# A block of unread products behind the last product of a streaming-encoder layer

## The chip, the core and the metric

The kernel runs on one core of a Trainium2 chip. TensorE (PE in the profile) multiplies a stationary operand, the weights, which is loaded into its array first (PEld), with a moving operand that is streamed through it column by column; results go into PSUM, eight accumulator banks. VectorE (DVE), ScalarE (ACT) and GpSimd (POOL) do everything elementwise; SyncE (SP) issues most of the DMAs. The metric is the device time of one execution in microseconds. Both kernels compute the same output; the change adds work whose results nothing reads.

## The reference

One layer on an input of 512 positions with 1024 channels, all in float32:

```python
h = rms_norm(x, norm_mix)
u_pool, u_lru, q, k, v, g_logits = split(h @ w_in)        # 8192 columns
gates = sigmoid(g_logits + b_gate)                        # three times 1024
y_pool = pool_mixer(u_pool)       # windows 2/4/8/16, grouped linear map
y_lru  = rglru_mixer(u_lru)       # causal convolution, gated scan over positions
y_sb   = stick_breaking_attention(rms_norm(q), rms_norm(k), v)   # 8 heads of 128
merged = gates0 * (y_pool @ wb0) + gates1 * (y_lru @ wb1) + gates2 * (y_sb @ wb2)
x = x + merged @ w_out
h2 = rms_norm(x, norm_ffn)
x = x + (silu(h2 @ w_gate) * (h2 @ w_up)) @ w_down        # 2816 hidden columns
```

## The kernel before

Everything is kept with channels on the 128 partitions and the 512 positions along the free dimension. A float32 matrix product is made of three products in the faster 32-bit matmul type float32r: each operand is split into a high part (a cast on ScalarE, L141, L1462) and a low part (the difference, on VectorE, L142, L1463), and high times high, high times low and low times high are accumulated (`mm3`, L304, and `product`, L310). In the attention's projection, in one branch and in the feed-forward part, the products of 2 by 2 blocks are made by a scheme with seven block products in place of eight; that is where the names "11", "S1" to "S4" and "22" come from.

The moving operand is not read in the order of its columns. `il` and `il2` (L94, L111) take the columns of the first and the second half of a block in turn, and whoever reads the result from PSUM puts them back in order:

```python
    def il2(ap):                                          # L111
        return ap.rearrange("p (a b) -> p b a", a=2)
```

So with 256 columns, neighbours in the stream lie 128 columns apart. The weights are always 128 neighbouring columns of a tile, such as `a_[a][:, w, k0 + k, :]`.

The last part is the down projection (L1681 on). For each of seven block products `nm` and both halves `q` of the output, `piece` (L1670) runs through three sets of weights and issues for each its products:

```python
                for k in range(nk):                       # L1675
                    for i, (a, b) in enumerate(((0, 0), (0, 1), (1, 0))):
                        nc.tensor.matmul(o, a_[a][:, w, k0 + k, :], il2(b_[b][:, k, :]),
                                         start=first and i == k == 0,
                                         stop=last and i == 2 and k == nk - 1, skip_group_check=True)
```

The sets of weights are prepared ahead by `make_d` (L1597): a cast `whd` or `whdS` on ScalarE and a difference `wld` or `wldS` on VectorE, each into one of a few rotating buffers, so the cast waits until TensorE has used up an older set. The very last piece, ("22", 1), is split by its two output blocks (L1686): after each, VectorE adds the result to the output tile (L1694) and SyncE stores it (L1652). The PSUM tiles `ps_dx`, `ps_dy` come from the pool `fp` with four tiles of two banks each; tiles of 128 by 1024 words in SBUF come from a rotating pool through `g4` (L1322). The framework that builds the program orders the instructions of each engine by priorities and sets the waits; each engine then works through its own list in order.

Of the kernel before, what the change touches and what calls it, by code (L numbers as in the profile page):

```python
# [8 lines left out]
F32 = mybir.dt.float32  # L9
F32R = mybir.dt.float32r  # L10
BF16 = mybir.dt.bfloat16
AF = mybir.ActivationFunctionType
# [4 lines left out]
P = 128  # L17
S = 512
# [46 lines left out]
def layer_kernel(ctx: ExitStack, tc: tile.TileContext, x, xt, vecs, w_in, w_qkv7, w_gate7, w_pool, w_rg, w_ig,  # L65
                 w_branch, w_br7, w_out, w_fg, w_fu, w_fd, w_fd7, out):
    nc = tc.nc
    act = nc.scalar.activation
    dve = nc.vector

    cst = ctx.enter_context(tc.tile_pool(name="cst", bufs=1))
    mp = ctx.enter_context(tc.tile_pool(name="mp", bufs=4))
# [46 lines left out]
    def two2(ap):  # L119
        if ap.shape[-1] == H:  # L120
            return ap.rearrange("p w (a b) -> p w a b", a=2)
        return ap.rearrange("p w (c a b) -> p (w c) a b", c=2, a=2)
# [314 lines left out]
    with ExitStack() as first:  # L437
# [288 lines left out]
        for k in range(KT):  # L726
            if k % 2 == 0:
                wh, wl = weights("first", k // 2)
            for w, x_ in ((wh, 0), (wl, 0), (wh, 1)):
                for n in range(4):  # L730
                    nc.tensor.matmul(pss[n // 2][n % 2], w[:, k % 2, n * P:(n + 1) * P], il(hu[k][x_]),  # L731
                                     start=k == 0 and w is wh and x_ == 0,
                                     stop=k == KT - 1 and x_ == 1)
# [46 lines left out]
        def store(t, i, j, r):  # L780
            nc.gpsimd.dma_start(rows(t, i, j), r)
# [115 lines left out]
        for cc in range(2):  # L897
# [14 lines left out]
            for nm in ORDER:  # L912
                ps, half, first_, t, ts_, src, ss = plan[nm]
# [328 lines left out]
    fp = ctx.enter_context(tc.tile_pool(name="fp", bufs=4, space=PSUM, reuse_waits="tile"))  # L1242
# [4 lines left out]
    with ExitStack() as third:  # L1247
# [42 lines left out]
        for u, nm in BORDER:  # L1290
# [5 lines left out]
            b = BH[nm]  # L1296
            for w in range(2):
                o = ps[:, w, half * H:(half + 1) * H]
                for k in range(4):
                    for n, (x_, y_) in enumerate(((0, 0), (0, 1), (1, 0))):  # L1300
                        nc.tensor.matmul(o, ah[x_][:, w, k, :], il2(b[k][y_]), start=first_ and n == k == 0,  # L1301
                                         stop=n == 2 and k == 3, skip_group_check=True)
# [16 lines left out]
    with ExitStack() as ffn:  # L1319
        gp = ffn.enter_context(tc.tile_pool(name="gp", bufs=GBUFS))  # L1320

        def g4(shape, name, dt=F32):  # L1322

            return gp.tile([P] + shape, dt, tag="g", name=name)
# [13 lines left out]
        for c in range(4):  # L1338
# [10 lines left out]
            for j in range(2):  # L1349
# [3 lines left out]
                t = x1p[c // 2, j][:, c % 2, :]  # L1353
# [112 lines left out]
        acts = []  # L1466
# [61 lines left out]
        for c in range(NDIRECT):  # L1528
# [4 lines left out]
            a = g4([2, S], f"act{c}")  # L1533
# [24 lines left out]
        for m in range(4):  # L1558
            t = fp.tile([P, 2, S], F32, tag="mm", name=f"ps_d{m}")
# [72 lines left out]
        for e in range(2):  # L1632
# [5 lines left out]
            for j in range(4):  # L1638
                m = 4 * e + j
# [41 lines left out]
        for nm in DORDER:  # L1681
# [3 lines left out]
            for q in range(2):  # L1685
                if (nm, q) == ("22", 1):  # L1686

                    make_d(len(dsets))
                    for w, ps in enumerate((XY[1, "y"], XY[0, "x"])):
# [3 lines left out]
                        t = two2(x1p[q, 1][:, ws, lo])  # L1693
# [15 lines left out]
                if nm == "22":  # L1709
                    store(q, 1, lo)  # L1710


_INS = ["x", "xt", "vecs", "w_in", "w_qkv7", "w_gate7", "w_pool", "w_rg", "w_ig", "w_branch", "w_br7", "w_out",
        "w_ffn_gate", "w_ffn_up", "w_ffn_down", "w_down7"]
# [43 lines left out]
```

## Time and profile before

| | us |
|---|---|
| time, median of two runs without profile | 868.24 (867.44 to 869.04) |
| span of the profiled execution, from its first to its last instruction | 866.1 |
| TensorE busy, products | 859.3 |
| TensorE busy, weight loads | 790.0 |
| VectorE busy | 735.4 |
| ScalarE busy | 523.1 |
| GpSimd busy | 91.1 |

The page gives a span for the profiled execution and no other time of it; the runs without profile are 2.1 us above it in the median. A row of the timeline has the start and the duration of an instruction in microseconds, engine, line, operation, `out<-in` by the program's names (for a product first the moving operand, then the weights), its shape, and in brackets how long its engine had been idle and who ended that. A matmul's duration is the time through the pipeline, with an end that is modelled, so the pace of TensorE is read from start to start. A group row has count, least, median and largest duration in ns, then the first and the last start.

### The profile page before, as it was taken

How to read it: one execution, taken by the hardware profiler on the slowest of the kernel's cores; microseconds unless marked ns; L12 is line 12 of the kernel's file. 1: busy time of each engine (PE TensorE's matmuls, PEld its weight loads, DVE VectorE, ACT ScalarE, POOL GpSimd, SP SyncE). 2: the span in 40 equal slices, each digit the busy share in tenths (PEclk: the TensorE clock that was granted, in tenths of full speed). 3: DMA queues.
4: the chain of work that ended last, by engine and by line, in shares of the span. 5: the costliest groups of instructions: out<-in, count | busy, mean ns of one | idle time of the engine just before them, and what ended most of it. 6: DMA issues, size and time to landing. Idle time of an engine off the chain costs nothing.

```text
span 866.1 us, 14232 instructions
## 1 busy us (share of the span) xinstructions
PE 859.3 (99%) x5563; PEld 790.0 (91%) x5563; DVE 735.4 (85%) x937; ACT 523.1 (60%) x727; POOL 91.1 (11%) x130
## 2 busy tenths in 40 slices
PE   9999999999999999999999999999999999999998
PEld 7888878888899988889889988889999999999998
DVE  7899897998796598967898786699988888899974
ACT  6554989556966567546665545465555555755642
POOL 1110002132433101000001100000000000121200
PEclk9999999999999999999999999999999999999999
DMA  9586346899592876735726955345533433797913
GB/s 340 160 284 208 101 156 186 225 315 264 172 313 74 240 222 195 243 119 157 222 87 169 202 165 172 101 139 148 159 110 98 122 99 123 225 243 195 197 42 122
DMA packets 116643, 154.08 MB, mean 178 GB/s; under 512 B 8160, under 2 KB 90080, under 8 KB 116576
## 3 DMA queue, kind: packets, MB, share of 16 engines
q1 hardware_dynamic: 103904, 107.30, 38.8%
q0 software_dynamic: 12528, 45.62, 22.2%
q8 instruction: 43, 0.70, 0.3%
q10 hardware_dynamic: 144, 0.26, 0.1%
q14 instruction: 24, 0.20, 0.1%
HBM read 132.71 MB, written 18.87 MB: 175 GB/s over the span
## 4 chain that ended last, share of the span: by engine, by line
PE 92%; ACT 4%; DVE 2%; issue 1%; DMA 0%; SPq 0%; DVEq 0%; ACTq 0%
PE ps_y L315 11%; PE ps_q L828 8%; PE ps_x L315 8%; PE ps_dy L1677 6%; PE ps_dx L1677 5%; PE ps_br L306 3%; PE ps_br L308 3%; PE ps_br L307 3%; PE ps_gate L731 3%; PE ps_bY L1301 2%; PE ps_gy L315 2%; PE ps_bX L1301 2%; PE ps_gx L315 2%; PE ps_pool L306 2%; PE ps_pool L307 2%; PE ps_pool L308 2%
## 5 line engine op out<-in xcount | busy, mean ns | idle before, releaser
L141 ACT ACTIVATE whi<-raw 128x1024 fp32r<-128x1024 f32 x69 | 72.8, 1055 | 81.7 <-PE ps_br L307 17.1
L142 DVE TENSOR_TENSOR wlo<-raw,whi 128x1024 fp32r<-128x1024 f32 x69 | 84.2, 1220 | 25.6 <-ACT whi L141 25.0
L142 DVE TENSOR_TENSOR wlo<-qw,whi 128x1024 fp32r<-128x1024 f32 x48 | 58.4, 1220 | 17.0 <-ACT whi L141 17.0
L141 ACT ACTIVATE whi<-qw 128x1024 fp32r<-128x1024 f32 x48 | 50.3, 1053 | 26.4 <-PE ps_q L828 11.9
L1462 ACT ACTIVATE wh_S<-w_S 128x1024 fp32r<-128x1024 f32 x36 | 38.4, 1066 | 28.6 <-PE ps_y L315 20.0
L1583 POOL DMA_DIRECT2D dw<-in_w_down_dram x20 | 17.0, 864 | 305.3 <-DVE wl L1463 242.6
L1463 DVE TENSOR_TENSOR wl_S<-w_S,wh_S 128x1024 fp32r<-128x1024 f32 x36 | 43.8, 1218 | 3.3 <-ACT wh_S L1462 3.3
L1462 ACT ACTIVATE wh<-w 128x1024 fp32r<-128x1024 f32 x27 | 28.6, 1060 | 29.3 <-PE ps_x L315 9.4
L1463 DVE TENSOR_TENSOR wl<-w,wh 128x1024 fp32r<-128x1024 f32 x27 | 32.9, 1219 | 7.8 <-ACT wh L1462 7.8
L1462 ACT ACTIVATE whdS<-dw 128x1024 fp32r<-128x1024 f32 x20 | 21.2, 1062 | 20.3 <-PE ps_dy L1677 10.6
L1113 DVE TENSOR_TENSOR_SCAN E<-K,ahead 128x512 f32<-128x512 f32 (+3 forms) x32 | 25.4, 813 | 5.7 <-ACT K L1109 5.6
L1463 DVE TENSOR_TENSOR wldS<-dw,whdS 128x1024 fp32r<-128x1024 f32 x20 | 24.2, 1220 | 4.9 <-ACT whdS L1462 4.9
L306 PE MATMUL ps_lru<-HH,whi 128*128 128x512 f32 x64 | 24.6, 384 | 0.0
L306 PE MATMUL ps_br<-yph,whi 128*128 128x512 f32 x64 | 24.5, 383 | 0.0
L306 PE MATMUL ps_pool<-HH,whi 128*128 128x512 f32 x64 | 24.5, 383 | 0.0
L306 PE MATMUL ps_br<-yHH,whi 128*128 128x512 f32 x64 | 24.5, 383 | 0.0
L306 PE MATMUL ps_gate<-HH,whi 128*128 128x512 f32 x64 | 24.4, 381 | 0.0
L307 PE MATMUL ps_lru<-HL,whi 128*128 128x512 f32 x64 | 24.3, 379 | 0.0
L308 PE MATMUL ps_lru<-HH,wlo 128*128 128x512 f32 x64 | 24.3, 379 | 0.0
L307 PE MATMUL ps_gate<-HL,whi 128*128 128x512 f32 x64 | 24.3, 379 | 0.0
L308 PE MATMUL ps_gate<-HH,wlo 128*128 128x512 f32 x64 | 24.3, 379 | 0.0
L307 PE MATMUL ps_pool<-HL,whi 128*128 128x512 f32 x64 | 24.3, 379 | 0.0
(740 smaller groups left out, 3437.2 us busy)
## 6 DMA issues: line engine op xcount, KB each, us to landing
raw<-in_w_in_dram SPq DMA_DIRECT2D x31, 512.0 KB, 5.2
qw<-in_w_qkv_dram SPq DMA_DIRECT2D x24, 512.0 KB, 6.9
dw<-in_w_down_dram POOLq DMA_DIRECT2D x20, 512.0 KB, 8.5
w<-in_w_ffn_gate_dram SPq DMA_DIRECT2D x36, 256.0 KB, 3.7
w<-in_w_ffn_up_dram SPq DMA_DIRECT2D x36, 256.0 KB, 4.6
raw<-in_w_branch_dram SPq DMA_DIRECT2D x16, 512.0 KB, 4.4
qw<-in_w_qkv_dram POOLq DMA_DIRECT2D x12, 512.0 KB, 7.6
qd<-r POOLq DMA_DIRECT2D x12, 512.0 KB, 7.2
```

The source lines that it names most:

```text
L141: act(hi, raw, AF.Copy)
L142: los.append(dve.tensor_tensor(lo, raw, hi.bitcast(F32), ALU.subtract).ins)
L306: nc.tensor.matmul(ps, lh, rh, start=start, stop=False, skip_group_check=skip)
L307: nc.tensor.matmul(ps, lh, rl, start=False, stop=False, skip_group_check=skip)
L308: nc.tensor.matmul(ps, ll, rh, start=False, stop=stop, skip_group_check=skip)
L315: nc.tensor.matmul(o, a_[a][:, w, k, :], il2(b_[b][:, k, :]), start=first and n == k == 0, stop=last and n == 2 and k == 3, skip_group_che ...
L731: nc.tensor.matmul(pss[n // 2][n % 2], w[:, k % 2, n * P:(n + 1) * P], il(hu[k][x_]), start=k == 0 and w is wh and x_ == 0, stop=k == KT - ...
L828: nc.tensor.matmul(ps[:, a, :], b_[:, k, ts_], il(a_[:, kk, :]), start=first and n == k == 0, stop=n == 2 and k == 3, skip_group_check=True)
L1301: nc.tensor.matmul(o, ah[x_][:, w, k, :], il2(b[k][y_]), start=first_ and n == k == 0, stop=n == 2 and k == 3, skip_group_check=True)
L1462: act(h, src, AF.Copy)
L1463: dve.tensor_tensor(l, src, h.bitcast(F32), ALU.subtract)
L1677: nc.tensor.matmul(o, a_[a][:, w, k0 + k, :], il2(b_[b][:, k, :]), start=first and i == k == 0, stop=last and i == 2 and k == nk - 1, skip ...
```

## The change

A function `probe` is added and called once, behind the loop of the down projection. It makes four tiles of 128 by 1024 words, two in float32r and two in plain float32, each a copy of one tile of activations on ScalarE. Then it issues 31 groups of products, 26 in float32r with 24 products each, 5 in plain float32 with 12 each. All products of a group write the same PSUM tile, each starting and stopping its own accumulation; nothing reads these tiles. A group is a pair of two choices, how the weights are read and how the moving operand is read:

- weights: `con(128)`, neighbouring columns; `step(s)`, every s-th column; `odd(s)`, every s-th from another offset; `same`, the same 128 columns each time; `off(n)`, neighbouring columns from an offset of n;
- moving operand: `con(n)`, n neighbouring columns; `way(n, a)`, n columns taken in turn from a equal parts, so that `way(256, 2)` is the order of `il2` with 256 columns.

```diff
@@ -67,6 +67,56 @@
     nc = tc.nc
     act = nc.scalar.activation
     dve = nc.vector
+
+    def probe(g4, fp, acts):
+        W, M = g4([2, S], "prw", F32R), g4([2, S], "prm", F32R)
+        W32, M32 = g4([2, S], "prw32"), g4([2, S], "prm32")
+        for t in (W, M, W32, M32):
+            act(t, acts[1], AF.Copy)
+        w, m = (t.rearrange("p a b -> p (a b)") for t in (W, M))
+        w32, m32 = (t.rearrange("p a b -> p (a b)") for t in (W32, M32))
+
+        def con(n):
+            return lambda t, i: t[:, n * (i % (1024 // n)):n * (i % (1024 // n)) + n]
+
+        def way(n, a):
+            f = con(n)
+            return lambda t, i: f(t, i).rearrange("p (a b) -> p b a", a=a)
+
+        def odd(s):
+            return lambda t, i: t[:, i % 8:][:, 0:128 * s].rearrange("p (c s) -> p c s", s=s)[:, :, 0]
+
+        def step(s):
+            def f(t, i):
+                v = t[:, 128 * s * (i // s % (8 // s)):][:, 0:128 * s]
+                return v.rearrange("p (c s) -> p c s", s=s)[:, :, i % s]
+            return f
+
+        def back(t, i):
+            return con(128)(t, i)[:, ::-1]
+
+        def off(n):
+            return lambda t, i: t[:, n + 128 * (i % 7):n + 128 * (i % 7) + 128]
+
+        def same(t, i):
+            return t[:, 0:128]
+
+        C, M2, M4, L2 = con(128), way(256, 2), way(256, 4), way(512, 2)
+        groups = [(C, M2), (step(2), M2), (step(4), M2), (step(8), M2), (odd(3), M2), (odd(5), M2), (odd(7), M2),
+                  (odd(6), M2), (same, M2), (off(16), M2), (off(32), M2), (off(64), M2), (C, con(256)),
+                  (step(2), con(256)), (step(8), con(256)), (C, M4), (step(2), M4), (step(8), M4), (C, way(256, 8)),
+                  (C, L2), (step(2), L2), (step(8), L2), (C, way(512, 4)), (C, con(128)), (step(2), con(128)),
+                  (step(8), con(128))]
+        plain = [(C, con(128)), (step(2), con(128)), (step(8), con(128)), (C, way(128, 2)), (C, M2)]
+        for g, (fw, fm) in enumerate(groups + plain):
+            tw, tm = (w, m) if g < len(groups) else (w32, m32)
+            n = 24 if g < len(groups) else 12
+            o = fp.tile([P, 2, S], F32, tag="mm", name=f"pr{g:02d}")
+            for i in range(n):
+                b = fm(tm, i)
+                cols_ = b.shape[1] * (b.shape[2] if len(b.shape) == 3 else 1)
+                nc.tensor.matmul(o[:, 0, 0:cols_], fw(tw, i), b, start=True, stop=True)
+
 
     cst = ctx.enter_context(tc.tile_pool(name="cst", bufs=1))
     mp = ctx.enter_context(tc.tile_pool(name="mp", bufs=4))
@@ -1709,6 +1759,8 @@
                 if nm == "22":
                     store(q, 1, lo)
 
+        probe(g4, fp, acts)
+
 
 _INS = ["x", "xt", "vecs", "w_in", "w_qkv7", "w_gate7", "w_pool", "w_rg", "w_ig", "w_branch", "w_br7", "w_out",
         "w_ffn_gate", "w_ffn_up", "w_ffn_down", "w_down7"]
```

On TensorE the list of before ends with the products of the down projection (L1677, names `ps_dx0` for the output, `Bd221h` and `Bd221l` for the moving operand, `whd224` and `wld224` for the weights):

```order
L1677 MATMUL ps_dx0_7994<-Bd221h_8709,whd224_9046 128x256
L1677 MATMUL ps_dx0_7994<-Bd221l_8710,whd224_9046 128x256
L1677 MATMUL ps_dx0_7994<-Bd221h_8709,wld224_9047 128x256
L1754 UNCONDITIONAL_BRANCH
```

In the changed program the groups follow at this place (`pr00` to `pr30` for the outputs, `prm`, `prw` and `prm32`, `prw32` for the tiles read):

```order
L1727 MATMUL ps_dx0_7994<-Bd221h_8709,wld224_9047 128x256
L118 MATMUL pr00_9136<-prm_9129,prw_9128 128x256 x24
L118 MATMUL pr01_9161<-prm_9129,prw_9128 128x256 x24
...
L118 MATMUL pr18_9586<-prm_9129,prw_9128 128x256 x24
L118 MATMUL pr19_9611<-prm_9129,prw_9128 128x512 x24
...
L118 MATMUL pr22_9686<-prm_9129,prw_9128 128x512 x24
L118 MATMUL pr23_9711<-prm_9129,prw_9128 128x128 x24
...
L118 MATMUL pr25_9761<-prm_9129,prw_9128 128x128 x24
L118 MATMUL pr26_9786<-prm32_9131,prw32_9130 128x128 x12
...
L118 MATMUL pr29_9825<-prm32_9131,prw32_9130 128x128 x12
L118 MATMUL pr30_9838<-prm32_9131,prw32_9130 128x256 x12
```

All that stood before them on TensorE keeps its order. On ScalarE, some 35 us before the end of the program before, casts of weights of the down projection (`whdS33` to `whdS41`) follow each other:

```order
L1462 ACTIVATE whdS33_8715<-dw113_7902 128x1024
L1483 ACTIVATE Bd222_8743<-act5_6507 128x512
L1462 ACTIVATE whdS34_8746<-dw114_7904 128x1024
L1462 ACTIVATE whdS40_8777<-dw210_7906 128x1024
L1462 ACTIVATE whdS41_8805<-dw211_7908 128x1024
```

In the changed program the four copies stand between them:

```order
L1512 ACTIVATE whdS33_8715<-dw113_7902 128x1024
L1533 ACTIVATE Bd222_8743<-act5_6507 128x512
L75 ACTIVATE prw_9128<-act1_5811 128x1024
L75 ACTIVATE prm_9129<-act1_5811 128x1024
L1512 ACTIVATE whdS34_8746<-dw114_7904 128x1024
L75 ACTIVATE prw32_9130<-act1_5811 128x1024
L75 ACTIVATE prm32_9131<-act1_5811 128x1024
L1512 ACTIVATE whdS40_8777<-dw210_7906 128x1024
L1512 ACTIVATE whdS41_8805<-dw211_7908 128x1024
```

The copies stand two and two ahead of the casts `whdS34` and `whdS40`; the rest of the list is the same. Lines of the changed kernel are 50 higher than those of before from L70 on.

## The prediction

> **What bounds the kernel now.** The page's head comes first, with the busy time of each engine and the clock in forty slices.
>
> ```profile
> span 866.1 us, 14232 instructions
> PE 859.3 (99%) x5563; PEld 790.0 (91%) x5563; DVE 735.4 (85%) x937; ACT 523.1 (60%) x727; POOL 91.1 (11%) x130
> PEclk9999999999999999999999999999999999999999
> ```
>
> TensorE works for 99% of the span, at the full granted clock in every slice. Whatever is put behind its last product therefore adds to the end unless something else already reaches further. Whether that is so is told by the chain that ended last (start, duration, what, how many instructions):
>
> ```profile
> 809.38 26.80 PE ps_dy L1677 x240
> 836.18 13.40 PE ps_dx L1677 x120
> 849.58 10.05 PE ps_dy L1677 x90
> 859.63 3.36 PE ps_dx L1677 x30
> 863.01 0.42 DVE x L1694
> ```
>
> The down projection (L1677) runs without a gap until 863, one VectorE add follows it, and then, in the timeline and in the list of DMA issues, one store:
>
> ```profile
> 862.70 0.28 PE L1677 MATMUL ps_dx<-Bd221h,wld 128*128 128x256 f32 x1
> 863.46 0.34 SPq L1652 DMA_DIRECT2D out_dram<-x  x1
> out_dram<-x SPq DMA_DIRECT2D x2, 128.0 KB, 1.7
> ```
>
> The store lands at about 863.46 + 1.7 = 865.2, and the span ends 0.9 us later. So at most 2.4 us (862.8 to 865.2) of added TensorE work can hide behind add and store.
>
> The first row of the chain also gives the pace of a 256-column product with its weight load: 26.80 / 240 = 0.1117 us.
>
> **The change part by part.** Nothing is removed. TensorE's order is the old one up to its last product, then come 31 groups (the words of the change say 32; the code's two lists hold 26 and 5). Counted by shape: 19 groups of 24 float32r products with 256 columns (456), 4 of 24 with 512 (96), 3 of 24 with 128 (72), and in plain fp32 4 groups of 12 with 128 columns (48) and one of 12 with 256. Each product has its own weight load.
>
> *256 columns.* 456 x 0.1117 = 50.9 us.
>
> *512 columns.* The timeline of TensorE at 29 us has these steps from start to start, and behind them the kernel's only plain fp32 products, four products with 128 columns (L522) that the trace shows as eight:
>
> ```profile
> 28.57 0.38 PE L307 MATMUL ps_gate<-hu,whi 128*128 128x512 f32 x1
> ...
> 29.43 0.38 PE L308 MATMUL ps_gate<-hu,wlo 128*128 128x512 f32 x1
> 29.65 1.05 PE L522 MATMUL rbps<-dg,ones 128*128 128x128 f32 x8
> L522 PE MATMUL rbps<-dg,ones x8: 273/275/275, 29.6 to 30.4; 128*128 128x128 f32 x8
> ```
>
> (29.65 - 28.57) / 5 = 0.216 us. 96 x 0.216 = 20.7 us.
>
> *Plain fp32.* Eight records take 1.05 us, of which the last is 0.275: (1.05 - 0.275) / 7 = 0.111 us from start to start, two to a product, so 0.221 us for 128 columns. Each record lasts 0.275, as long as a float32r product with 256 columns (0.28 above), so it streams twice its columns. 48 x 0.221 = 10.6 us. With 256 columns I double the columns, and take 2 x 0.216 for one: 12 x 0.432 = 5.2 us.
>
> *128 columns in float32r.* No row shows this shape. By its columns alone it would take a quarter of 0.216, 0.054 us; the weight load has its own floor, which shows where TensorE has been idle and two loads follow each other:
>
> ```profile
> 553.06 0.19 PEld L1374 LDWEIGHTS ps_rms<-sqh,onesr 128*128 128x128 f32 x1 [0.49 <-ACT sqh L1371]
> 553.06 0.49 PE L1374 MATMUL ps_rms<-sqh,onesr 128*128 128x512 f32 x1
> 553.16 0.19 PEld L308 LDWEIGHTS ps_fg<-h2h,wlo 128*128 128x128 f32 x1
> 327.70 1.25 PE L1126 MATMUL pw<-idn,A 128*128 128x128 f32 x10
> L1126 PE MATMUL pw<-idn,A x80: 272/273/273, 327.7 to 455.6; 128*128 128x128 f32 x80
> ```
>
> The second load starts 0.10 us after the first though nothing else is left to wait for. I take the load as the limit, at the 0.111 of the fp32 records: 72 x 0.111 = 8.0 us, with 72 x 0.054 = 3.9 as the lower end. [...]
>
> *Sum.* 50.9 + 20.7 + 10.6 + 5.2 + 8.0 = 95.4 us.
>
> *Order of the moving columns.* In before, nearly all moving operands are read in pairs from two places (`il`, `il2`: neighbours are 128 columns or more apart). Three groups read 256 columns in a row instead. The kernel has that once, in L1374 above; beside it stands the longest of the paired ones that also started on an idle engine:
>
> ```profile
> L1374 PE MATMUL ps_rms<-sqh,onesr x1: 495/495/495, 553.1 to 553.1; 128*128 128x512 f32 x1
> L306 PE MATMUL z<-qkh,qkh x32: 272/328/483, 303.7 to 449.1; 128*128 128x256 f32 x16, 128*128 128x512 f32 x8, 128*128 128x384 f32 x8
> ```
>
> That is 12 ns more for 512 columns in a row. For 256 I take half, 6 ns, less the 3 ns by which the load (0.1117) outlasts the columns: the transposes of L1126, each as long as a 256-column product, follow each other by (1.25 - 0.273) / 9 = 0.109, the nearest row for the columns alone. 72 x 3 ns = 0.2 us. Four and eight interleaved places (M4, 256 by 8, 512 by 4) have no row; I take them at the pace of two, between nothing and double time, 96 x 0.11 + 24 x 0.21 = 15.6 us.
>
> *Weights at steps.* Every load of before reads neighbouring columns. Below: if a step made loads faster, a 256-column product could fall to 0.109, at most 456 x 0.003 = 1.4 us. Above: a load that takes twice its 0.111. 17 of the 31 groups have a step over 1. Steps of 4 or more columns occur in 192 float32r loads whose product has 256 or 128 columns and in 24 plain ones: 216 x 0.111 = 24.0 us; steps 2 and 3 in 144 more, 16.0 us. (With 512 columns even a doubled load, 0.22, is hidden but for 0.01.) I take nothing, because the nearest row is again the moving operand: it takes a column every 0.216 / 512 = 0.42 ns with each neighbour 1 KB away, and a load needs only one column every 0.111 / 128 = 0.87 ns.
>
> *The four copies on ScalarE.* They stand ahead of two casts of weights, where the engine waits for buffers:
>
> ```profile
> 825.38 1.07 ACT L1462 ACTIVATE whdS<-dw 128x1024 fp32r<-128x1024 f32 x1 [0.58 <-PE ps_dy L1677]
> 826.36 0.61 ACT L1483 ACTIVATE Bd<-act 128x512 fp32r<-128x512 f32 x1
> 828.06 1.06 ACT L1462 ACTIVATE whdS<-dw 128x1024 fp32r<-128x1024 f32 x1 [1.09 <-PE ps_dy L1677]
> 830.74 1.06 ACT L1462 ACTIVATE whdS<-dw 128x1024 fp32r<-128x1024 f32 x1 [1.62 <-PE ps_dy L1677]
> 831.84 1.23 DVE L1463 TENSOR_TENSOR wldS<-dw,whdS 128x1024 fp32r<-128x1024 f32 x1 [0.26 <-ACT whdS L1462]
> 833.42 1.06 ACT L1462 ACTIVATE whdS<-dw 128x1024 fp32r<-128x1024 f32 x1 [1.62 <-PE ps_dy L1677]
> 833.33 0.28 PE L1677 MATMUL ps_dy<-BdS31h,whdS 128*128 128x256 f32 x1
> ```
>
> At 1.06 us each, two copies run 827.0 to 829.1, the cast of 828.06 moves to 829.1, two more copies follow it, and the cast of 830.74 moves to 832.3, 1.6 late; the one of 833.42 is then on time. Queued behind are those casts and their VectorE differences, for which TensorE waits. The product at 833.33 is, by program order, the first to read the cast of 828.06; a set of weights lasts 24 products, 24 x 0.1117 = 2.7 us, so the cast of 830.74 is first read at 836.0 and its difference at about 836.2. The difference ended at 833.06, now at about 834.7: 1.5 us are left, cost nothing. Without that cover TensorE would stall by the 1.6. VectorE moves one add by one place, SP and POOL issue the same DMAs in the same order.
>
> *The end.* The first added product starts at 862.70 + 0.11 = 862.8; the first group needs no result of the add at 863.01, and its 2.7 us outlast add and accumulator. TensorE ends at 862.8 + 95.4 + 0.2 + 0.2 (the last product's tail) = 958.6, and with the same 0.9 us to the end of the span: 959.5. Runs without profile stand 868.24 - 866.1 = 2.1 above this span, so the time is 961.6, rounded to 962 us, 94 more than before.
>
> **The rivals.**
>
> *Weights at wide steps load slower.* A load that fetches a separate place for every column may take longer than one in a row; against it stands the moving operand's row, for it that no load of before has a step, and loads are already the limit at 256 columns (0.1117 against 0.109). Doubled from step 4 on: 962 + 24 = 986; from step 2 on: 1002. [...] Chance 0.20.
>
> *More than two interleaved places are slow to stream.* If the reader keeps just two places open, the 96 products with 256 and 24 with 512 columns double: 962 + 15.6 = 978. The trace has two places only, so it says nothing against it but that the distance makes no difference (the products of `z`, quoted above, read 64 columns apart and last 272 at least, L1677's read 128 apart). Chance 0.10.
>
> *Faster than the sum.* Loads in float32r overlap more than L1374 shows, or steps speed them up: 962 - 4.1 - 1.4 = 956.5. Chance 0.08.
>
> *Not slower: the unread products are not executed.* Nothing reads `pr`; if whatever builds the program leaves out what nobody reads, TensorE ends at 863 again and the time is 868. Place: all 31 groups; price: the whole 95; it decides once fewer than about a sixth of them are left (17.4 of 95 us). TensorE's order in the built program has all of them, so 0.01.
>
> **How the numbers follow.** The forecast, 962, has 0.59, with 957.5 to 968 for itself, where loads that lose some nanoseconds per step are inside. The remaining 0.02 is for a stall that none of these cover. From 956 to 986 lie the forecast, the faster case, the many places, and the first half of the slow loads, about 0.85. Two per cent is 17.4 us, about what a measurement of this kernel tells from no change; all cases but the left-out products are above it: faster 0, same 0.01, slower 0.99.
>
> **What would show it.** In the profile after: 744 more TensorE records (624 + 2 x 60); L1677 ends at 863 as before, so that the copies cost nothing; then, group by group, 24 products in 2.7 us for 256 columns, 5.2 for 512, 2.7 for 128, and 12 in 2.7 for plain fp32 with 128. A group `pr` whose steps are at 0.22 names the rival: the second to eighth for steps of weights, the sixteenth to nineteenth and the twenty-third for places. The three 128-column groups show the load alone; near 1.3 us each would prove me wrong there. What would make it wrong most is a load whose time depends on the step.

## The result, and the profile after

| | before | after |
|---|---|---|
| time, median of two runs each, us | 868.24 (867.44 to 869.04) | 1000.37 (999.80 to 1000.93) |
| ratio | | 1.1529 [1.1510, 1.1548] |
| span of the profiled execution | 866.1 | 999.1 |

The change costs 132 us where 94 were forecast; 1000.4 lies above the range of 956 to 986. The page's head and the chain of waits of the changed kernel (chain: start, duration, what, how many):

```profile
span 999.1 us, 15725 instructions
PE 994.6 (100%) x6307; PEld 919.6 (92%) x6307; DVE 735.3 (74%) x937; ACT 526.4 (53%) x731; POOL 89.6 (9%) x130
PEclk9999999999999999999999999999999999999998
835.86 13.40 PE ps_dx L1727 x120
849.26 10.05 PE ps_dy L1727 x90
859.31 3.35 PE ps_dx L1727 x30
862.66 135.51 PE pr L118 x744
```

TensorE has 744 more records, as forecast. The old work ends at 862.66 (863.0 before) and its pieces keep their lengths, so nothing is lost ahead of the probe. The whole miss is in the last row: 135.5 us instead of 95.4. One digit at the end of the clock row is an 8, which before did not show.

All groups of the probe run at one source line and one tile name. They are told apart here by windows: each row below is the stretch from the first product of a group to that of the next, then TensorE's busy time (in brackets the records that touch the window, neighbours included), the granted clock, the DMA share and GB/s. A group of 24 products (plain fp32: 12 products, two records each) at the forecast's pace takes 2.68 us, or 5.18 with 512 columns.

```profile
862.50:865.18 2.68, 2.68 (x25) 1.00 0.14 49
865.18:868.05 2.87, 2.87 (x27) 1.00 0.00 0
868.05:873.67 5.62, 5.62 (x26) 1.00 0.00 0
873.67:879.43 5.76, 5.76 (x25) 1.00 0.00 0
879.43:883.66 4.23, 4.23 (x25) 1.00 0.01 4
883.66:889.05 5.39, 5.39 (x26) 1.00 0.00 0
910.75:913.62 2.87, 2.87 (x27) 1.00 0.00 0
922.27:925.70 3.43, 3.43 (x25) 1.00 0.02 5
934.81:940.14 5.33, 5.33 (x26) 1.00 0.00 0
956.35:963.11 6.76, 6.76 (x26) 1.00 0.00 0
963.11:965.74 2.63, 2.63 (x25) 1.00 0.00 0
968.57:974.33 5.76, 5.76 (x26) 0.88 0.00 0
974.33:979.56 5.23, 5.23 (x26) 0.50 0.01 3
982.46:988.17 5.71, 5.71 (x27) 1.00 0.00 0
```

In this order: weights in a row, at steps of 2, 4, 8, 3 and 5, all with 256 columns from two places; then weights in a row again, with 256 columns in a row, from four and from eight places, with 512 columns from four places, and with 128 columns. The last three are 128 columns with weights at step 8, and then plain fp32: in a row, and with weights at step 8.

Three things stand out. Weights at step 3 take 1.58 times as long as in a row, and from step 4 on about twice. Four and eight places of the moving columns also take longer, up to twice. And one group of the plainest kind, plain fp32 in a row, took 5.23 us while the clock was at 0.50. Repeating the same weights, or starting them 16, 32 or 64 columns further on, costs nothing: these four groups take 2.68 us each.

### The profile page after: what moved, and what is told of

Read it like the earlier page. It is cut to its first block, busy times and chain, and to the rows that moved or that the text cites. A ratio compares the mean times of both kernels' runs of the same rounds, so it can differ in the third digit from the quotient of the medians.

```text
span 999.1 us, 15725 instructions
## 1 busy us (share of the span) xinstructions
PE 994.6 (100%) x6307; PEld 919.6 (92%) x6307; DVE 735.3 (74%) x937; ACT 526.4 (53%) x731; POOL 89.6 (9%) x130
## 4 chain that ended last, share of the span: by engine, by line
PE 93%; ACT 3%; DVE 2%; issue 1%; DMA 0%; SPq 0%; DVEq 0%; ACTq 0%
PE pr L118 14%; PE ps_y L365 10%; PE ps_q L878 7%; PE ps_x L365 7%; PE ps_dy L1727 5%; PE ps_dx L1727 4%; PE ps_br L356 3%; PE ps_br L358 3%; PE ps_br L357 3%; PE ps_gate L781 2%; PE ps_bY L1351 2%; PE ps_gy L365 2%; PE ps_bX L1351 2%; PE ps_gx L365 2%; PE ps_pool L357 1%; PE ps_pool L356 1%
## 5 line engine op out<-in xcount | busy, mean ns | idle before, releaser
L118 PE MATMUL pr<-prm,prw 128*128 128x256 f32 (+2 forms) x744 | 135.7, 349 | 0.0
L118 PEld LDWEIGHTS pr<-prm,prw 128*128 128x128 f32 x744 | 129.8, 245 | 5.5
L191 ACT ACTIVATE whi<-raw 128x1024 fp32r<-128x1024 f32 x69 | 72.8, 1055 | 82.1 <-PE ps_br L357 17.1
L358 PE MATMUL ps_br<-yHH,wlo 128*128 128x512 f32 x64 | 24.3, 379 | 0.0
L357 PE MATMUL ps_br<-ypl,whi 128*128 128x512 f32 x64 | 24.3, 379 | 0.0
```

The costliest lines, as they stand in the source:

```text
L118: nc.tensor.matmul(o[:, 0, 0:cols_], fw(tw, i), b, start=True, stop=True)
L191: act(hi, raw, AF.Copy)
L357: nc.tensor.matmul(ps, lh, rl, start=False, stop=False, skip_group_check=skip)
L358: nc.tensor.matmul(ps, ll, rh, start=False, stop=stop, skip_group_check=skip)
```

## The experiments

In all of them what differs lies behind the last product and is unread, so the layer's output is the one before; only the run that puts the columns of the kernel before in a row is without a probe. Each probe has one run, set beside the kernel before on the same chip (medians of 867 to 868 us), so what a change costs is read from the groups in its profile. Paces are from start to start, the mean within a group, or the median where single starts stand out.

**Weights in a row, columns as they are.** Every group of the changed kernel gets neighbouring weights.

```diff
+        groups, plain = ([(C, fm) for _, fm in gs] for gs in (groups, plain))
```

> All 31 groups read their weights as neighbouring columns, the moving orders stay. Theory of the lines: a weight load costs about 1.83 ns for each 16-byte line that its 128 columns touch, and at least 0.108 us, so the stepped groups fall to the pace of the unstepped ones with the same moving order: 12 x 2.68 + 3 x 2.87 + 3 x 3.43 + 5.33 + 3 x 5.2 + 6.76 + 3 x 2.64 + plain 3 x 5.2 + 3.28 + 6.56 = 112.0 us for the groups in place of 135.5, about 977 us. If the extra came from elsewhere (clock, order, queue), the time stays near 1000.

The 1.83 ns are an estimate from the changed kernel: 234 ns a product at step 4 (5.62 us / 24) over 128 columns. That stretches of 16 bytes, four such columns, are the unit is assumed, because step 8 (5.76 us) costs hardly more than step 4. "Line" means such a stretch here.

Measured: 969.59 us, probe 104.7 us. Windows of that run, for the group that had step 4 with 256 columns, then eight places, 128 columns (step 8 in the changed kernel), and plain fp32 in a row:

```profile
867.35:870.03 2.68, 2.68 (x26) 1.00 0.00 0
913.10:918.43 5.33, 5.33 (x26) 1.00 0.00 0
940.79:943.42 2.63, 2.63 (x26) 1.00 0.00 0
948.78:951.51 2.73, 2.73 (x27) 1.00 0.03 6
```

Every group that had a step falls to the pace without one: together 28.3 us. The time is 7 below the 977 expected, because of plain fp32: in a row it takes 2.73 us here and took 5.23 in the changed kernel, though this group's weights were in a row there too. I had booked 5.2 to plain fp32 in three groups, and each of them takes 2.7.

**Weights as they are, columns in two places.** The float32r groups with 256 and 512 columns all get the order of before.

```diff
+        fixed = []
+        for fw, fm in groups:
+            n = fm(m, 0)
+            n = n.shape[1] * (n.shape[2] if len(n.shape) == 3 else 1)
+            fixed.append((fw, {256: M2, 512: L2}.get(n, fm)))
+        groups = fixed
```

> The weights keep their steps; every float32r group with 256 or 512 columns reads the moving operand from two places. If the moving orders are a cost of their own, beside that of the steps: contiguous, four-place and eight-place groups fall to 2.68 us with unstepped weights and stay at 2.87 and 5.76 with steps 2 and 8; all groups 129.8 us in place of 135.5, about 995 us. If slow orders were slow only together with stepped loads, the gain would be near 0.

Measured: 993.44 us, probe 128.4 us, 7 less than 135.5. Windows of the groups that had eight places with 256 columns and four places with 512, both with weights in a row:

```profile
932.98:935.66 2.68, 2.68 (x25) 1.00 0.00 0
951.82:957.00 5.18, 5.18 (x25) 1.00 0.00 0
```

With weights in a row, the groups of 256 columns in a row, from four and from eight places fall to 2.68 us, 512 columns from four places from 6.76 to 5.18. The orders of the columns are a second, smaller cost beside the steps. They are 5.7 of the 7 us; most of the rest, 1.3, lies in the first plain group, of which less fell under the halved clock (3.94 us instead of 5.23).

**Both.** Weights in a row everywhere, float32r columns in two places, plain columns in a row.

```diff
+        cols = lambda fm: fm(m, 0).shape[1] * (fm(m, 0).shape[2] if len(fm(m, 0).shape) == 3 else 1)
+        groups = [(C, {128: con(128), 256: M2, 512: L2}[cols(fm)]) for _, fm in groups]
+        plain = [(C, con(cols(fm))) for _, fm in plain]
```

> All 31 groups with weights in a row, the float32r groups with 256 and 512 columns in two places, the plain ones in a row; the same 744 products by shape, unread as before. If the whole miss lies in the order of the weights and of the columns (and in the clock that the slow loads brought down), the probe lasts what the prediction's sum says without its 0.2 for the order of columns: 50.9 + 20.7 + 8.0 + 10.6 + 5.2 = 95.4 instead of 135.5 us, and the time is 1000.4 - 40.1 = 960.3. Rival: something else in the groups also costs, for example a group's first product or a change of shape; then more than 1 us remains above that.

This was run last, when the paces of the other runs were known. Measured: 960.47 us. The last row of its chain:

```profile
862.13 95.58 PE pr L123 x744
```

With the orders out, the forecast's sum holds to 0.2 us. So the miss is closed: between this run and the one with weights in a row lie 9.1 us of orders of columns, between that and the changed kernel 28.3 of steps and 2.5 in the one group at half clock; 95.6 + 9.1 + 28.3 + 2.5 = 135.5.

**Loads by themselves.** Why do steps cost? Either a load is slow on its own, or it hinders the stream of columns that runs beside it. 17 groups of 24 float32r products, most with only 16 columns.

```diff
-        groups = [(C, M2), (step(2), M2), (step(4), M2), (step(8), M2), (odd(3), M2), (odd(5), M2), (odd(7), M2),
...
+        groups = [(same, T), (every(2), T), (every(2, 1), T), (every(3), T), (every(3, 1), T), (every(4), T),
+                  (every(4, 2), T), (every(5), T), (every(6), T), (every(7), T), (every(8), T), (same, con(128)),
+                  (every(8), con(128)), (every(8), con(256)), (every(8), M2), (every(8), L2), (every(4), way(256, 8))]
```

> Weight loads with a product of only 16 columns behind each, so that no long moving stream runs beside the load; then step 8 with 128, 256 and 512 columns. Lines: from load to load 0.108 us in a row, 0.118 at step 2, 0.176 at step 3 (96 lines), 0.225 to 0.24 from step 4 on, whatever the product; all groups 82 us, about 947 us. Rival, collision with the moving operand's reads: with 16 columns every step is at 0.11, and only the last groups are slow; about 925 us.

Measured: 954.71 us. Windows with 16 columns and weights in a row, at steps 2 (from the next column on), 3, 4 and 8, then 128 columns with weights in a row and at step 8, and step 8 with 512 columns:

```profile
862.48:865.08 2.60, 2.60 (x25) 1.00 0.15 50
869.19:874.31 5.12, 5.12 (x26) 0.50 0.00 0
874.31:879.43 5.12, 5.12 (x26) 0.50 0.00 0
884.55:890.13 5.58, 5.58 (x25) 0.50 0.00 0
911.92:917.63 5.71, 5.71 (x25) 0.50 0.01 3
917.63:922.79 5.16, 5.16 (x25) 0.50 0.00 0
922.79:928.53 5.74, 5.74 (x25) 0.50 0.00 0
940.18:946.07 5.89, 5.89 (x25) 1.00 0.01 3
```

A load at step 8 takes as long with 16 columns beside it (5.71) as with 128 (5.74) or 512 (5.89), and as in the changed kernel (5.76). So the columns don't matter: the load alone is slow. The clock fell to 0.50 here, among these short products, and that gives a second result: loads in a row, which took 111.7 ns, and at steps 2 and 3 now stand at 213 ns, but steps 4 and 8 stay at 233 and 238, the paces they have at full clock (5.62 and 5.76 us in the changed kernel). The raised floor is also why the time is 8 us above the 947 expected. The floor of a row nearly doubled with the clock at 0.50 and the cost of steps 4 and 8 stayed. That the fetching of the weights is behind this is a guess; no run shows it.

**The order of the columns.** Weights fixed and in a row, 512 columns in float32r in 18 orders, and three groups of fewer columns.

```diff
+        groups = [(same, con(512)), (same, pairs(2)), (same, pairs(4)), (same, pairs(8)), (same, pairs(16)),
+                  (same, pairs(32)), (same, pairs(64)), (same, pairs(128)), (same, way(512, 2)), (same, way(512, 4)),
+                  (same, way(512, 8)), (same, way(512, 16)), (same, runs(2, 2)), (same, runs(4, 2)), (same, runs(8, 2)),
...
```

> Weights always the same neighbouring columns, moving operand of 512 columns in many orders. Lines, of which two may be open: in a row 0.239 us (128 lines of 1.87 ns), pairs at a distance of 2 columns (within a line) 0.239, pairs at 4 to 256 columns 0.216, four places 0.282, eight and sixteen 0.445, four or eight places in runs of two columns 0.223, runs of four 0.216 to 0.24, every second column 0.478, 256 columns at step 4 0.478, 128 at step 8 0.24, 384 in a row 0.18. Rival, banks of the memory by address: distances differ among themselves (some of 4 to 256 as slow as in a row), and sixteen places are no slower than four.

Measured: 1007.34 us. Windows of 512 columns in a row, in pairs 4 columns apart, 256 apart, from four and eight places, and from two places two columns at a time:

```profile
862.35:867.84 5.49, 5.49 (x24) 1.00 0.07 24
873.28:878.46 5.18, 5.18 (x25) 1.00 0.00 0
904.36:909.54 5.18, 5.18 (x25) 1.00 0.00 0
909.54:916.33 6.79, 6.79 (x26) 1.00 0.00 0
916.33:928.00 11.67, 11.67 (x25) 1.00 0.00 1
...
938.46:946.35 7.89, 7.89 (x25) 1.00 0.00 0
```

Pairs take 215.9 ns a product at every distance from 4 to 256 columns; at 2 they take 226.7, about what a row takes. So the distance of the two places made no difference from 4 columns (16 bytes) on. Four places take 283, eight 487, sixteen 435. If at most two lines could be held open and each new one cost 1.87 ns (estimated from the changed kernel's 2.87 us for 24 products of 256 columns in a row, 64 lines each), a row would take 239 (227 measured) and two places by twos 216 (328 measured). No rule that I formed fits all rows. A price per 16-byte line does not either: a row (128 lines) and every second column (256 lines, 451 ns) both cost about 1.77 ns a line, but every fourth of 256 columns (256 lines) takes 233 ns, where 478 was expected, and every eighth of 128 columns (128 lines) 111, where 240 was. A row costs about 11 ns more than pairs at all three lengths: 256 columns 119.7 against the 109 of the columns alone, 384 columns 173 against three quarters of 215.9, 162, and 512 columns 227 against 216.

**Shifted columns, and plain fp32.** Both operands in a row, the moving one shifted by 0 to 512 columns against the weights. Is the cost of a row that weights and columns fall on the same place? And is plain fp32 in a row always at 213 ns a record?

```diff
+        groups = [(same, at(256, o)) for o in (0, 4, 8, 16, 32, 64, 128)] + [(same, at(128, o)) for o in (0, 128)]
+        plain = [(same, at(128, o)) for o in (0, 1, 2, 4, 8, 12, 16, 24, 32, 64, 128, 256, 512)]
+        plain += [(same, lambda t, i: t[:, 0:128].rearrange("p (a b) -> p b a", a=2)),
...
```

> Weights and moving operand both read in a row, the moving one shifted by 0 to 512 columns against the weights (their tiles lie whole multiples of 4 KB apart); 9 groups float32r, 18 in plain fp32. Theory of the lockstep: the two streams of a plain product run at the same pace, and where both meet the same part of the memory each waits for the other: 0.213 us from record to record at shift 0, and 0.111, the pace of the kernel's own plain products, at some of the shifts. Rival: plain fp32 in a row costs 0.213 wherever it lies. In float32r 256 columns in a row: 0.120 at every shift if it is the lines alone.

Measured: 947.21 us. Windows of 256 float32r columns in a row without shift and shifted by 16, then plain fp32 with 128 columns in a row without shift, from two places, and with 256 in a row:

```profile
861.82:864.69 2.87, 2.87 (x25) 1.00 0.13 46
870.35:873.07 2.72, 2.72 (x26) 1.00 0.00 0
886.97:889.70 2.73, 2.73 (x26) 1.00 0.00 0
921.86:925.14 3.28, 3.28 (x26) 1.00 0.00 0
933.78:938.97 5.19, 5.19 (x25) 1.00 0.00 0
```

Plain fp32 in a row takes 111.7 ns a record at every one of the 13 shifts, and float32r stays at 117 to 120 but for the shift of 16 (113.5, only 4 to 5 ns above the columns alone). Neither idea holds, though that one shift shows that the place of a row against its weights has some part in its price. Plain fp32 has the other preference: two places are slower than a row there (136.7 against 111.7 with 128 columns; with 256, 273 in the changed kernel against 215.8 here), where in float32r they are faster (215.9 against 227 with 512 columns).

**Plain groups first.** Then why 5.23 us in the changed kernel? The clock at 0.50 begins within the group before it, 128 columns with weights at step 8.

```diff
-        for g, (fw, fm) in enumerate(groups + plain):
-            tw, tm = (w, m) if g < len(groups) else (w32, m32)
-            n = 24 if g < len(groups) else 12
+        for g, (fw, fm) in enumerate(plain + groups):
+            tw, tm = (w, m) if g >= len(plain) else (w32, m32)
+            n = 24 if g >= len(plain) else 12
```

> The five plain fp32 groups are run ahead of the 26 fp32r groups; nothing else is changed, and the results of the probe stay unread. Theory: the first plain group took 213 ns a record in the changed kernel because the TensorE clock was at half behind the group of step 8 with 128 columns, and not because of plain fp32. Then plain 128 columns in a row take 111.7 ns a record here (2.7 us for the group), the clock falls only behind the last group, where little is left, and the time is 1000.4 - 2.5 = 998. Rival: the first plain group pays for a change of the type of the products; then its pace stays at 213 ns and the group at 5.2 us wherever it stands, and the time stays at 1000.

Measured: 997.74 us. Windows of the first plain group and of the last group, 128 float32r columns with weights at step 8:

```profile
861.94:864.62 2.68, 2.68 (x25) 1.00 0.15 49
989.04:995.01 5.97, 5.97 (x26) 0.77 0.00 0
```

The group takes 2.68 us at full clock, and the clock now falls at the end, again within that group of short products behind slow loads. The 2.5 us are the clock's.

**bf16.** If 16 bytes are the unit, as assumed so far, bf16 should pay at twice the step. 24 products of 256 columns for each step.

```diff
+        groups = [(same, T), (every(2), T), (every(3), T), (every(4), T), (every(5), T), (every(6), T), (every(7), T),
+                  (every(8), T), (same, way(256, 2)), (every(4), way(256, 2)), (every(8), way(256, 2))]
```

> The probe is replaced by eleven groups of 24 products of 128 bf16 weights by 256 bf16 columns: weights at steps of 1, 2, 3, 4, 5, 6, 7 and 8 with the columns in a row, then steps 1, 4 and 8 with the columns in two places. Eight bf16 columns lie in 16 bytes, where four fp32 columns do. Theory of lines: a load costs 1.83 ns for each 16 bytes that it touches, or the stream of the columns if that is longer (0.11 to 0.12 us). Steps 2 and 3 (32 and 48 lines) are then hidden, step 4 (64 lines) gives 0.118, 5 (80) 0.146, 6 (96) 0.176, 7 (112) 0.205, 8 (128) 0.234 us a product. Rival, cost by columns skipped: as with fp32, 0.118 at step 2, 0.176 at step 3 and 0.234 us from step 4 on.

Measured: 903.72 us. All eight steps stand at 109.1 ns: both forecasts wrong, no step shows. What costs is the order of the columns, 243.4 ns from two places.

**bf16 loads by themselves.** 64 columns, so that the load is the limit; then orders of columns.

```diff
+        T = con(64)
+        groups = [(same, T), (every(2), T), (every(3), T), (every(4), T), (every(5), T), (every(6), T), (every(7), T),
+                  (every(8), T), (same, con(512)), (same, way(512, 2)), (same, way(512, 4)), (same, way(512, 8)),
+                  (same, nth(2)), (same, nth(4)), (same, nth(8))]
```

> bf16 again, eight groups of 24 products with 64 columns, weights at steps of 1 to 8, and then seven with weights in a row and 512 columns (in a row; in two, four and eight places; every second), 256 (every fourth) and 128 (every eighth). With 256 columns no step showed; a weight load itself lasted 98 ns at steps 1 and 2, 113 at step 4 (64 lines of 16 bytes) and 143 at step 8 (128 lines), which is 30 ns for 64 lines. Theory: the load of bf16 costs 0.47 ns a line, a quarter of the 1.83 of fp32, and at least the stream, 64 x 0.42 = 27 ns; that is 27 to 30 ns up to step 4, 37 at step 5, 45 at 6, 52 at 7 and 60 ns at step 8. Rival: a load of bf16 does not depend on the step; then all eight groups stay at one pace. Moving columns: two places took 243 ns for 256 columns, 0.95 ns a column. If each change of the line costs that, 512 columns give 487 ns in two, four and eight places, and 216 for every second (128 lines). If it is the step of the columns that costs, every second gives 487 too, and every eighth 122.

Measured: 949.33 us. Windows of 64 columns with weights in a row and at step 8, then 512 columns in a row, from two and from four places:

```profile
862.12:862.83 0.71, 0.71 (x24) 1.00 0.00 0
...
868.40:869.84 1.44, 1.44 (x28) 1.00 0.00 0
869.84:875.02 5.18, 5.18 (x27) 1.00 0.00 0
875.02:886.65 11.63, 11.63 (x26) 1.00 0.00 0
886.65:907.38 20.73, 20.73 (x26) 0.54 0.00 1
```

The pace is 29.1 ns for steps 1 to 3, then 33.3, 40.1, 46.7, 53.3 and 60.0 for steps 4 to 8, as the theory of lines had it within 4 ns. In the run before, all of this was hidden behind the 109 ns of the columns. At full spread a bf16 load thus costs a quarter of a float32r load (60 against 234 to 240). In a row it takes at most 29 ns, against 112: 64 columns need 27 themselves (an eighth of the 215.9 for 512 in a row), so the load may be shorter still. Why the factor is about 3.9 at full spread, no run shows.

For the columns neither theory held. Two places gave the 484 expected, but four gave 864 and eight 861, where one theory had 487 for both. The clock fell to 0.50 soon after the four places began, but their first product, before that, already took 849. Every second of 512 columns (at full clock), every fourth of 256 and every eighth of 128 all gave 226.7, neither the 109 to 122 of one theory nor a cost by column. Each of these three touches 128 lines of 16 bytes, so these three fit a price by the line, 226.7 / 128 = 1.77 ns, and not by the column; every eighth kept it at a clock of 0.50 too.

**The order in the kernel before.** Without a probe: do 12 ns for a row, whatever its length, hold in the kernel itself? `il` and `il2` leave the columns in a row, and the results are read so too.

```diff
     def il2(ap):
-        return ap.rearrange("p (a b) -> p b a", a=2)
+        return ap
```

> The kernel before without the added groups, with every moving operand read in a row and results taken from PSUM in a row. If 256 columns in a row cost 0.120 in place of 0.112 us and 512 cost 0.239 in place of 0.216 everywhere: 3098 x 8 ns + 2150 x 23 ns = 74 us more, about 942 us. If only the 12 ns for 512 columns hold that the one such product of before showed: 3098 x 6 + 2150 x 12 ns = 44 us more, about 912 us. If the order does not matter to products in the kernel: 868 us.

Measured: 922.73 us (922.31 to 923.66), ratio to before 1.0633 [1.0613, 1.0654]. TensorE is still the limit:

```profile
PE 916.7 (100%) x5563; PEld 814.4 (88%) x5563; DVE 739.2 (80%) x937; ACT 525.3 (57%) x727; POOL 89.3 (10%) x130
```

From start to next start, the mean of all products with 512 columns became 231.1 ns (218.1 before) and that of all with 256 120.1 (111.9): 2243 x 13.0 ns = 29 and 3119 x 8.2 ns = 26, together 55 us. No order tried is faster than that of before, which is worth 6% of this kernel's time. A row has a price per product that hardly depends on its length: 13 ns at 512 columns, and at 256 the 11 less the 3 that the load covers.

## Why the prediction was wrong

**What held.** By shape, in us; the last column is the run with both orders plain, whose plain products are in a row:

| | forecast | changed kernel | orders taken out |
|---|---|---|---|
| float32r, 256 columns, 456 products | 50.9 | 77.6 | 50.9 |
| float32r, 512 columns, 96 | 20.7 | 23.0 | 20.7 |
| float32r, 128 columns, 72 | 8.0 | 11.2 | 8.0 |
| plain fp32, 128 columns, 48 | 10.6 | 17.1 | 10.8 |
| plain fp32, 256 columns, 12 | 5.2 | 6.6 | 5.2 |

Every pace that came from a row of before held to 0.2 us, also the 128 columns in float32r, for which the load was taken as the limit. The probe started at 862.5 (forecast 862.8), the span ended 0.9 us after the last product, as before, and the median stood 1.3 above the span (2.1 taken). The copies cost nothing, for the reason given:

```profile
831.30 1.04 ACT L1512 ACTIVATE whdS<-dw 128x1024 fp32r<-128x1024 f32 x1
832.37 1.23 DVE L1513 TENSOR_TENSOR wldS<-dw,whdS 128x1024 fp32r<-128x1024 f32 x1 [0.76 <-ACT whdS L1512]
835.92 0.28 PE L1727 MATMUL ps_dx<-BdS40h,wldS 128*128 128x256 f32 x1
```

The cast that was to be 1.6 us late started 0.56 later than before (830.74), since copies follow each other in 0.95 us and not 1.06. Its difference ended at 833.6, and the third product of the set, the first to read it, starts at 835.92 (last row): 2.3 us of cover left (1.5 forecast).

**The step that failed: "I take nothing, because the nearest row is again the moving operand".** It was a wrong neighbour. The time of a float32r load fits 1.83 ns for each 16-byte line it touches, as soon as that exceeds the 111.7 of a row: 64 lines 117.8 ns (step 2), 96 lines 176 (step 3), 128 lines 234 (step 4), and from there on nothing more (224 to 240 for steps 5 to 8). The moving operand with its columns from two places pays nothing for that (215.9 ns with 512 columns). The argument from the rate, one column every 0.87 ns, compared a demand with what another reader delivers. Cost of this step: 28.3 us, of which 25.7 at steps of 4 and more (24.0 in the rival), 1.6 at step 3, and the rest at step 2 and with 512 columns. The rival "weights at wide steps load slower" was right, but its 986, the end of the range, has doubled loads from step 4 on and nothing for steps 2 and 3. No run had shown that split; the runs then showed 5% more than in a row at step 2, 58% more at step 3, and about double from step 4 on.

**The rivals were made alternatives.** "More than two interleaved places are slow to stream" was right too: its 120 products cost 6.5 us with weights in a row (four places with 256 columns 2.3, eight 2.65, four with 512 columns 1.6), where 15.6 were allowed for doubling, and 5.5 in the changed kernel, whose slow loads cover a part. Nothing in either rival excluded the other, yet each was added to 962 alone, and the range ended at the first. Both together were 962 + 24.0 + 15.6 = 1001.6, which lies 1.2 us above the time partly by chance: the steps cost more than that, the places less, and the clock isn't in it. Two independent rivals with 0.20 and 0.10 had a joint case that belonged in the working, and the slow loads deserved more than 0.20, since the only evidence against them was a row of another reader.

**Smaller terms.** For a row of 256 columns I halved the 12 ns of 512; the price is about 11 at either length, so the three groups cost 8 ns a product instead of 3, where no step hides it. The plain products with columns from two places were priced as in a row: 12 with 128 columns 0.6 and 12 with 256 columns 1.4 us more. And the halved clock, 2.5 us in one group, had no place in the forecast at all: I read the full clock of the kernel before as given.

**What stays open.** Why the loads fit 1.83 ns a line, and why steps 5, 6 and 7 (224, 224 and 233 ns) lie below step 8 (240) though all four touch 128 lines. Why a float32r stream in a row is about 11 ns a product slower than pairs, why plain fp32 and bf16 are the other way round, and what sets 283, 487 and 435 ns for four, eight and sixteen places. Distance between two places, a clash with the weights' place and a limit of two open lines were each tried and don't explain the rows; the clash has a part at most, by the one shift of 16.

## What to carry to other kernels

Price a float32r weight load as these runs fit it: the larger of its 111.7 ns in a row and 1.83 ns for each 16 bytes it touches, so such weights should be neighbours (or every second at most, 117.8 ns), and only a product of 512 columns hid most of a scattered load (242 ns against 216). Which order of the moving columns is fast depended on the type: in float32r take two places (215.9 ns against 227 in a row, 512 columns), in plain fp32 and bf16 a row (111.7 a record against 136.7 with 128 columns, 109.1 against 243.4 with 256). And when two rivals touch different terms, price them together as well as apart.

## What the runs showed of the hardware that was not expected

- **A scattered load did not slow with the clock.** At a granted clock of 0.50, in the run of the loads by themselves, loads in a row went from 111.7 to 213.3 ns, loads at steps 4 and 8 stayed at 233 and 238.
- **The clock halved under products that never paused.** It fell to 0.50 where the columns stream for little of the time, taking 216 / 512 = 0.42 ns a column: 128 columns behind loads of 240 ns (22%), 128 bf16 columns, every eighth, in 226.7 (24%), 512 bf16 columns from four places in 864 (25%), 16 columns behind 112 (6%). It stayed at 1.00 where the share was 45% (256 columns behind 240 ns; 512 bf16 columns from two places in 484). In the changed kernel it lasted 6.8 us, by the windows at 0.88, 0.50 and 0.97. TensorE's busy time fills those windows (5.23 of 5.23 us at 0.50), so in these groups the lower clock went with the share of streaming, not with pauses between instructions.
- **bf16 from two places took 2.2 times as long as in a row** (243.4 against 109.1 ns for 256 columns), the opposite of float32r (111.7 against 119.7).
